# A hybrid decoder layer on one core: moving work from VectorE and GpSimd to ScalarE and to accumulating DMAs, and turning the attention-value product round

## The chip, the cores and the metric

The kernel runs on one core of a Trainium2 chip. The metric is device time in microseconds, the median of repeated runs. One further execution was taken by the hardware profiler; all rows below come from it.

## The reference

One layer works on a residual stream x of 1024 positions by 1024 channels. A conditioning vector c gives six vectors (shift, scale and gate for two sub-layers). The first sub-layer normalises x and makes one projection into state-space channels, eight query heads, two key heads and two value heads:

```python
h = _rms(x, norm1_w) * (1 + sc1) + sh1
u, q, k, v = split(h @ w_in)
y_ssm = _s5(u, ...)          # 32 groups, complex state of 64, scan over positions, GELU, GLU
y_attn = _swa_sink(rms(q), rms(k), v, rel_bias, sinks)   # 8 heads, window of 128, blocks of 128
mixed = concat([_rms(y_ssm, out_norm_ssm), _rms(y_attn, out_norm_attn)])
x = x + g1 * (mixed @ w_out)
h2 = _rms(x, norm2_w) * (1 + sc2) + sh2
x = x + g2 * _conv_ffn(h2, w_up, conv_w, conv_b, w_down)   # width 3 convolution, SiLU gate
```

The attention's softmax divides each row of exponentials by its sum plus the exponential of a learned sink:

```python
probs = p / (sum(p) + exp(sink - m));  out = probs @ v_band
```

## The kernel before

The residual stream is kept transposed: channels on partitions, positions on columns, in eight tiles x[0] to x[7] of 128 by 1024. A half h is 512 positions. All large matmuls run as `mm3` (line 143): each operand is split into a rounded part and a remainder (`split`, line 137), and three products are summed in one PSUM bank. In a split, one engine writes the rounded part (ScalarE unless named otherwise) and another the remainder (VectorE unless named otherwise). Helpers such as `tt`, `stt`, `cpy` issue most instructions, so a line of the profile (L118, L127, L133, L135, L97, L99) is often that of a helper, and the tiles tell the groups apart.

The stages in order of time are these. The adaLN vectors are made by VectorE (`emit_mod`, line 178), which reduces a loaded tile of w_mod against c (L180). The state-space input U is projected, and `emit_ut` (line 539) transposes it in eight groups of four 128-column blocks into one PSUM bank each, from where VectorE moves it to SBUF and adds a bias Bu (L118, tA<-bk,Bu). The heads' projections and the scan follow, the scan on VectorE. The scan's outputs go through a GELU on ScalarE, are transposed by TensorE into eight banks and moved to the tile zT (line 735, tS<-bk, four by ScalarE and four by VectorE). They are split (line 746, the rounded part by VectorE, tA<-tS) and pass the GLU (L770, L775).

Attention (lines 810 to 856) runs over eight blocks n of 128 queries and two key heads kv, in 16 units u. A unit makes the logits of four heads (tXQ,tH), adds the bias and takes the row maximum on VectorE (L828), takes exponentials on ScalarE with the row sum (L837), and takes the reciprocal of the sum plus sink (L840). Then P is multiplied by that reciprocal, on GpSimd in 14 units and on VectorE in two (the list `PM`; tH<-tH,att). P is transposed (cn,tH or cn,tA), the transposes are moved to PT by ScalarE or VectorE in turn (the list `EP`; tH<-bk, 15 of 30 by each), and the product with V follows:

```python
pe.matmul(av[kv * 64:kv * 64 + 64, :], vtok[...64 columns...], PT[:, kb * 512:kb * 512 + 512], ...)
```

V is stationary (64 columns) and the transposed probabilities of four heads move (512 columns), so channels come out on partitions. Each block's result is moved by two ScalarE copies of 128x256 (tU<-bk). P has three buffers, H4, H5 and A12.

After four blocks `branch_norm(h)` (line 788) normalises the attention branch: four squares on ScalarE, three sums on VectorE, a matmul with ones, a reciprocal square root over 128x512, four products on VectorE, four splits.

`proj` (line 882) makes one 128x512 piece of the output projection and adds it, times the gate g1, to x by one VectorE instruction (L127, tX<-bk,mod,tX or tXQ<-bk,mod,tXQ). Line 863 has loaded x before, in eight transfers of 512 KB issued by SyncE. The state-space share (br_i = 0) comes first, in the order d = 4 to 7 with both halves and then d = 0 to 3 with the first half; the second halves of d = 0 to 3 follow later. Its pieces use bank 5 for the first half and bank 6 for the second. The weights come through one staging buffer, W0. The attention share is added by `attn_out` (line 986) with `proj(d, h, 1, ...)`, which also stores x to DRAM and takes squares; `rms` (line 1003) normalises for the second sub-layer.

The order on each engine is made by a scheduler that simulates the kernel; attention has raised priority (line 807), and `attn_out` for the first half is held behind the last unit's reciprocal (line 1017). From there TensorE's order is that of the program text (L99, against L97 before). Sixteen `emit_mod` of the second sub-layer are held behind units 10 to 15 (the list `MOD_AT`, line 906). Each queue is served in its order, DMA issues included. The second sub-layer then keeps TensorE busy to the end.

## Time and profile before

| what | value |
|---|---|
| median of 3 runs | 1140.12 us (1139.39 to 1141.47) |
| the profiled execution's own time | 1142.15 us |
| span of the profiled execution | 1140.3 us |
| mean granted TensorE clock | 0.958 of full speed |

In the rows, PE is TensorE, PEld its weight loads, DVE is VectorE, ACT is ScalarE, POOL is GpSimd, SP is SyncE. "bk" is a PSUM bank. A busy time is the time in which an instruction of the engine, or of the group, was running; successive instructions overlap a little, so a mean times a count exceeds it slightly. PEclk is the mean granted clock, 1.00 for 2.4 GHz and 0.50 for 1.2 GHz. One 32-bit matmul appears as two records. A GpSimd instruction's span includes time in which it could not get on.

### The profile page before, as it was taken

The page shows a single profiled execution, that of the slowest core. Times are in us where ns is not written, and L with a number is a line of the kernel's source. Part 1 is how long each engine was busy: PE and PEld are TensorE (multiplying, and loading weights), DVE is VectorE, ACT ScalarE, POOL GpSimd, SP SyncE. Part 2 cuts the span into 40 slices and gives each one's busy share as a digit, 9 for nine tenths or more (in the row PEclk, how much of TensorE's full clock was granted, in tenths as well). Part 3 has the DMA queues.
Part 4 walks back from the last instruction along what each step waited for, and adds up shares of the span by engine and source line. Part 5 has one row for each costly group of instructions (what it writes and reads, how often), then busy time and mean ns, then how long its engine had stood idle before and what let it go on. Part 6 is the DMA issues. An engine that isn't in the chain of part 4 may idle for free.

```text
span 1140.3 us, 13281 instructions
## 1 busy us (share of the span) xinstructions
PE 1053.4 (92%) x4692; PEld 828.2 (73%) x4692; DVE 957.5 (84%) x1541; ACT 550.2 (48%) x936; POOL 256.7 (23%) x137
## 2 busy tenths in 40 slices
PE   6979999688989899779999999999999989989998
PEld 4868777475646577657888888888888768768876
DVE  8996899969988988888777878797777787997985
ACT  5412443583874346745554545455444554434342
POOL 0000000002121001762122223212212142353541
PEclk9979999679989899989999999999999989999999
DMA  9501516025024743222223232423123359120002
GB/s 371 214 19 39 127 40 93 1 88 190 19 94 183 240 147 112 93 92 93 93 78 113 87 130 93 151 90 112 56 93 126 115 217 384 63 93 1 1 37 111
DMA packets 47333, 128.13 MB, mean 112 GB/s; under 512 B 6017, under 2 KB 13985, under 8 KB 47266
## 3 DMA queue, kind: packets, MB, share of 16 engines
q1 hardware_dynamic: 47266, 127.28, 32.8%
q8 instruction: 37, 0.61, 0.2%
q14 instruction: 30, 0.25, 0.1%
HBM read 105.28 MB, written 21.99 MB: 112 GB/s over the span
## 4 chain that ended last, share of the span: by engine, by line
PE 60%; DVE 29%; ACT 4%; DMA 3%; issue 3%; POOL 1%; SPq 0%; ACTq 0%; DVEq 0%; POOLq 0%
PE bk L97 54%; PE bk L99 6%; DVE tA L118 5%; DVE tU L118 3%; DVE tH L118 3%; DVE tS L118 2%; DVE tX L127 2%; DMA tW<-in_dram 2%; DVE bk L118 2%; DVE tS L180 1%; DVE tXQ L118 1%; DVE tXQ L127 1%; DVE tX L118 1%; DVE tX L180 1%; ACT tU L133 1%
## 5 line engine op out<-in xcount | busy, mean ns | idle before, releaser
L97 PE MATMUL bk<-tU,tU 128*128 128x512 f32 x516 | 124.9, 395 | 4.8 <-DVE tXQ L127 2.4
L97 PE MATMUL bk<-tA,tU 128*128 128x512 f32 x516 | 128.1, 395 | 0.8 <-DVE tA L118 0.8
L97 PEld LDWEIGHTS bk<-tU,tU 128*128 128x128 f32 x516 | 97.6, 190 | 27.8 <-issue 2.8
L97 PE MATMUL bk<-tH,tU 128*128 128x512 f32 x477 | 116.0, 392 | 0.0
L97 PEld LDWEIGHTS bk<-tA,tU 128*128 128x128 f32 x516 | 96.7, 188 | 24.2 <-DVE tA L118 1.4
L127 DVE SCALAR_TENSOR_TENSOR tX<-tH,sm,tX 128x1023 f32<-128x1023 f32 x66 | 100.5, 1523 | 8.0 <-ACT tX L1097 7.9
L97 PEld LDWEIGHTS bk<-tH,tU 128*128 128x128 f32 x477 | 89.1, 188 | 19.3
L97 PE MATMUL bk<-tA,tXQ 128*128 128x512 f32 x300 | 76.0, 401 | 2.1 <-ACT tH L1050 2.1
L118 POOL TENSOR_TENSOR tU<-tW,tU 128x512 fp32r<-128x512 f32 x25 | 36.3, 1462 | 174.1 <-ACT tU L133 152.4
L97 PE MATMUL bk<-tH,tA 128*128 128x512 f32 (+1 forms) x168 | 63.9, 509 | 11.4 <-ACT tH L133 7.6
L133 ACT CAST tU<-tW 128x512 fp32r<-128x512 f32 (+1 forms) x67 | 47.1, 710 | 48.9 <-PE bk L97 18.2
L97 PEld LDWEIGHTS bk<-tA,tXQ 128*128 128x128 f32 x300 | 57.4, 191 | 16.0 <-ACT tH L1050 2.5
L99 PE MATMUL bk<-tH,tU 128*128 128x512 f32 x267 | 64.0, 395 | 1.8 <-DVE tU L118 1.7
L118 POOL TENSOR_TENSOR tH<-tH,att 128x1024 f32<-128x1024 f32 (+1 forms) x9 | 19.1, 2124 | 195.8 <-DVE att L840 161.7
L118 DVE TENSOR_TENSOR tX<-tX,tX 128x512 f32<-128x512 f32 (+1 forms) x63 | 61.6, 981 | 0.8
L118 POOL TENSOR_TENSOR tXQ<-tW,tXQ 128x512 fp32r<-128x512 f32 x12 | 49.1, 4102 | 53.1 <-ACT tXQ L133 37.8
L99 PEld LDWEIGHTS bk<-tH,tU 128*128 128x128 f32 x267 | 49.6, 189 | 15.6 <-DVE tU L118 2.7
L97 PE MATMUL bk<-tXQ,tH 128*128 128x256 f32 (+2 forms) x224 | 51.9, 374 | 4.3 <-DVE att L828 4.3
L118 DVE TENSOR_TENSOR tU<-tW,tU 128x512 fp32r<-128x512 f32 (+2 forms) x43 | 37.8, 881 | 20.4 <-ACT tU L133 20.4
L97 PEld LDWEIGHTS bk<-tXQ,tH 128*128 128x128 f32 x224 | 45.1, 268 | 13.3 <-DVE att L828 9.0
L118 POOL TENSOR_TENSOR tU<-tX,tU 128x512 fp32r<-128x512 f32 x19 | 33.2, 1747 | 84.9 <-ACT tU L133 70.8
L118 DVE TENSOR_TENSOR tU<-tX,tU 128x512 fp32r<-128x512 f32 x39 | 31.3, 808 | 23.6 <-ACT tU L133 23.6
(349 smaller groups left out, 2398.9 us busy)
## 6 DMA issues: line engine op xcount, KB each, us to landing
tX<-in_dram SPq DMA_DIRECT2D x51, 512.0 KB, 3.3
tW<-in_dram SPq DMA_DIRECT2D x49, 512.0 KB, 3.3
tS<-in_dram SPq DMA_DIRECT2D x30, 512.0 KB, 6.0
gd<-tX SPq DMA_DIRECT2D x22, 512.0 KB, 2.9
tA<-in_dram SPq DMA_DIRECT2D x12, 512.0 KB, 9.7
tH<-in_dram SPq DMA_DIRECT2D x12, 512.0 KB, 4.2
tH<-gd SPq DMA_DIRECT2D x8, 512.0 KB, 4.7
tA<-gd SPq DMA_DIRECT2D x8, 512.0 KB, 8.9
```

What stands on the lines that cost most here:

```text
L97: return f(*a, **k)
L99: i = f(*a, **k)
L118: return eng.tensor_tensor(out=o, in0=a, in1=b, op=op)
L127: return vec.scalar_tensor_tensor(out=o, in0=a, scalar=s, in1=b, op0=op0, op1=op1)
L133: act.copy(o, i)
L180: vec.tensor_tensor_reduce(out=st, in0=st, in1=ca, scale=1.0, scalar=S("b_mod", j, 1), op0=MUL, op1=ADD, accum_out=mod[:, j:j + 1],)
```

## The change

The change does six things. First, the eight bias moves of `emit_ut` go from one VectorE instruction each to four ScalarE instructions of 128x128. Second, in the list `PICK` all eight moves to zT go to ScalarE, the eight rounded parts of zT's split too, and of the 30 moves to PT VectorE keeps three. Third, P is no longer multiplied by the reciprocal; the product with V has PT as the stationary operand (128 columns) and V moving (64 columns), in eight matmuls a unit (four in the first two), so queries come out on partitions, and one VectorE instruction of 128x512 a block multiplies by the reciprocals. ScalarE then takes the row sum of squares into a junk output in the second unit's P buffer. Fourth, `branch_norm` works from these sums: a reciprocal square root over 128x4, four ScalarE scalings, 16 transposes into bank 7 (first half) or banks 0 to 3, and from the bank four ScalarE moves and four VectorE remainders. Fifth, `proj` for the state-space share writes g1 times the product to x by ScalarE, and a DMA issued by GpSimd adds the 256 KB of x from DRAM to it, in 16 transfers. Sixth, the eight loads of x by SyncE are gone.

```diff
-    "EI": "a", "EK": "a", "EP": "avavavavavavavavavavavavvaav", "ET": "a", "EU": "avaaavaa", "EV": "a", "EW": "a",
-    "EZ": "av", "NS0": "a", "NS1": "aav", "PM": "pppvppppp", "QH": "a", "ZH": "v", "YB": "67566556",
+    "EI": "a", "EK": "a", "EP": "aaaaaaaav", "EU": "avaaavaa", "EV": "a", "EW": "a",
+    "EZ": "a", "NS0": "a", "NS1": "aav", "QH": "a", "ZH": "a", "YB": "67566556",
...
-        tt(vec, v4[0], v4[1], Bu[:, 4 * i:4 * i + 4].rearrange("p (g o) -> p g o", o=1).to_broadcast([128, 4, 128]), ADD)
+        for q in range(4):
+            g = 4 * i + q
+            act.activation(out=UTt[i // 2][:, (g % 8) * 128:(g % 8 + 1) * 128], in_=b[:, q * 128:(q + 1) * 128], func=AF.Identity, bias=Bu[:, g:g + 1])
...
     def branch_norm(h):
...
+        ssq, rs, tm = [att[:, 128 * h + 4 * z:128 * h + 4 * z + 4] for z in range(3)]
+        rsqrt_mean(rs, tm, ssq, 512)
+        for j in range(4):
+            act.activation(out=Y[h][j], in_=Y[h][j], func=AF.Identity, scale=rs[:, j:j + 1])
         for m in range(4):
+            b = bank[m if h else 7]
+            for j in range(4):
+                pe.transpose(b[:, j * 128:(j + 1) * 128], Y[h][j][:, m * 128:(m + 1) * 128], ident)
+            hi, lo = mx[4 + m, h] = half(newr(f"H{8 + 4 * h + m}"))
+            act.activation(out=hi.r, in_=b, func=AF.Identity, scale=bw[:, 4 + m:5 + m])
+            stt(lo.r, b, bw[:, 4 + m:5 + m], hi.f, MUL, SUB)
...
-            tt(ENG[pick("PM", u)], P, P, rd.rearrange("p (i o) -> p i o", o=1).to_broadcast([128, 4, w_]), MUL)
...
-            for kb in range(nb):
-                blk = (n - 1 + kb) if n else 0
-                pe.matmul(av[kv * 64:kv * 64 + 64, :], vtok[:, blk * 128 + kv * 64:blk * 128 + kv * 64 + 64],
-                          PT[:, kb * 512:kb * 512 + 512], start=(kb == 0), stop=(kb == nb - 1))
+            for i in range(4):
+                for kb in range(nb):
+                    blk = (n - 1 + kb) if n else 0
+                    pe.matmul(av[:, (2 * i + kv) * 64:(2 * i + kv) * 64 + 64], PT[:, kb * 512 + i * 128:kb * 512 + i * 128 + 128],
+                              vtok[:, blk * 128 + kv * 64:blk * 128 + kv * 64 + 64], start=(kb == 0), stop=(kb == nb - 1))
...
+        tt(vec, g8[0], g8[1], att[:, 256 + 8 * n:264 + 8 * n].rearrange("p (g o) -> p g o", o=1).to_broadcast([128, 8, 64]), MUL)
+        act.activation(out=Pt[:, 0:512], in_=y, func=AF.Square, accum_out=att[:, 128 * (n // 4) + n % 4:128 * (n // 4) + n % 4 + 1])
...
-    for k in range(8):
-        sync.dma_start(out=x[k], in_=xT[k])
...
+        if br_i == 0:
+            i = act.activation(out=x[d][:, hs], in_=b, func=AF.Identity, scale=g1)
+            pol.dma_start(out=x[d][:, hs], in_=xT[d][:, hs], accum_op=ADD)
+            return i
         return stt(x[d][:, hs], b, g1, x[d][:, hs], MUL, ADD)
```

## Rows read from the trace of the kernel before

**Rows 1.** The page: busy time of each engine, and the ending chain by engine.
```profile
PE 1053.4 (92%) x4692; PEld 828.2 (73%) x4692; DVE 957.5 (84%) x1541; ACT 550.2 (48%) x936; POOL 256.7 (23%) x137
...
PE 60%; DVE 29%; ACT 4%; DMA 3%; issue 3%; POOL 1%; SPq 0%; ACTq 0%; DVEq 0%; POOLq 0%
```

**Rows 2.** Windows: stretch, its length, busy PE, PEld, DVE, ACT, POOL, PEclk, DMA.
```profile
94.00:111.00 17.00, 16.24 (x133) 13.97 (x133) 12.09 (x36) 5.35 (x9) 0.00 (x0) 1.00 0.12 39
...
235.00:257.00 22.00, 16.66 (x103) 13.71 (x102) 13.18 (x37) 18.98 (x51) 2.17 (x3) 0.77 0.35 120
257.00:273.00 16.00, 11.90 (x55) 7.24 (x52) 16.00 (x43) 3.48 (x13) 1.80 (x1) 1.00 0.53 178
273.00:330.00 57.00, 50.56 (x213) 33.14 (x214) 51.54 (x127) 44.37 (x113) 15.44 (x7) 0.88 0.19 62
330.00:382.00 52.00, 51.57 (x217) 31.92 (x215) 44.43 (x100) 23.82 (x61) 10.57 (x4) 1.00 0.54 191
382.00:402.00 20.00, 14.68 (x52) 10.76 (x52) 17.75 (x33) 7.66 (x12) 0.00 (x0) 0.83 0.73 239
402.00:457.00 55.00, 53.43 (x231) 42.96 (x231) 45.78 (x64) 30.92 (x47) 5.70 (x4) 1.00 0.36 126
```

**Rows 3.** Groups of VectorE, 235 to 400 us: busy, mean ns, idle before.
```profile
L135 DVE COPY tH<-bk 128x512 f32<-128x512 f32 x15 | 10.2, 679 | 0.2 <-PE bk L97 0.2
L127 DVE SCALAR_TENSOR_TENSOR tS<-tU,tS 128x512 f32<-128x512 f32 x8 | 8.7, 1104 | 0.0
...
L127 DVE SCALAR_TENSOR_TENSOR tX<-bk,mod,tX 128x512 f32<-128x512 f32 x8 | 5.8, 742 | 4.1 <-PE bk L97 4.1
...
L135 DVE COPY tS<-bk 128x512 f32<-128x512 f32 x4 | 4.4, 1104 | 2.7 <-PE bk L97 2.7
...
L135 DVE CAST tA<-tS 128x512 fp32r<-128x512 f32 x8 | 3.0, 417 | 1.6 <-ACT tS L133 1.6
```

**Rows 4.** The timeline of GpSimd and VectorE: start, length, instruction, idle before.
```profile
289.51 2.16 POOL L118 TENSOR_TENSOR tH<-tH,att 128x1024 f32<-128x1024 f32 x1 [7.75 <-DVE att L840]
...
289.84 2.38 DVE L127 SCALAR_TENSOR_TENSOR tS<-tU,tS 128x512 f32<-128x512 f32 x1
...
469.29 31.15 POOL L118 TENSOR_TENSOR tXQ<-tW,tXQ 128x512 fp32r<-128x512 f32 x1 [5.30 <-ACT tXQ L133]
```

**Rows 5.** The timeline of TensorE and VectorE near 390 us.
```profile
387.79 2.95 PE L97 MATMUL bk<-tA,tHA 128*128 128x512 f32 x12
395.98 4.85 PE L97 MATMUL bk<-tA,tHA 128*128 128x512 f32 x12 [5.24 <-DVE tXQ L127]
...
395.18 0.74 DVE L127 SCALAR_TENSOR_TENSOR tXQ<-bk,mod,tXQ 128x512 f32<-128x512 f32 x1
```

**Rows 6.** Groups of ScalarE, 235 to 400 us: busy, mean ns, idle before.
```profile
L133 ACT COPY tH<-bk 128x512 f32<-128x512 f32 x15 | 8.7, 580 | 6.5 <-PE bk L97 6.0 <-ACT tU L133 0.5
...
L770 ACT ACTIVATE tU<-bk,bg 128x512 f32<-128x512 f32 x8 | 5.3, 675 | 0.5 <-PE bk L97 0.5
...
L133 ACT COPY tU<-bk 128x256 f32<-128x256 f32 x16 | 5.1, 372 | 9.1 <-PE bk L97 9.1
...
L133 ACT COPY tS<-bk 128x512 f32<-128x512 f32 x4 | 4.4, 1095 | 0.0
L133 ACT CAST tU<-tW 128x1024 fp32r<-128x1024 f32 x3 | 3.1, 1048 | 10.0 <-DMA tW<-in_dram 10.0
```

**Rows 7.** The timeline of TensorE's 32-bit matmuls (stationary 128*64 or 128*128, then moving).
```profile
284.93 1.93 PE L97 MATMUL bk<-tH,tA 128*64 128x512 f32 x4
...
240.10 0.39 PE L97 MATMUL bk<-tA,tS 128*128 128x128 f32 x2
240.32 0.39 PE L97 MATMUL bk<-tHB,tA 128*128 128x128 f32 x2
```

**Rows 8.** DMA issues, 230 to 470 us: count, KB each, median us to landing.
```profile
tXQ<-in_dram SPq DMA_DIRECT2D x4, 512.0 KB, 5.2
...
xd<-tX SPq DMA_DIRECT2D x8, 256.0 KB, 2.1
```

More of the change, by code (lines that the diff above doesn't have):

```diff
@@ L38 @@
 PICK = {
-    "EI": "a", "EK": "a", "EP": "avavavavavavavavavavavavavvaav", "ET": "a", "EU": "avaaavaa", "EV": "a", "EW": "a",
-    "EZ": "av", "NS0": "a", "NS1": "aav", "PM": "pppvppppp", "QH": "a", "ZH": "v", "YB": "67566556",
+    "EI": "a", "EK": "a", "EP": "aaaaaaaav", "EU": "avaaavaa", "EV": "a", "EW": "a",
+    "EZ": "a", "NS0": "a", "NS1": "aav", "QH": "a", "ZH": "a", "YB": "67566556",
 }
@@ L545, in emit_ut @@
             pe.transpose(b[:, q * 128:(q + 1) * 128], U[:, g * 128:(g + 1) * 128], ident)
-        v4 = [a_.rearrange("p (g c) -> p g c", g=4) for a_ in (UTt[i // 2][:, (i % 2) * 512:(i % 2 + 1) * 512], b)]
-        tt(vec, v4[0], v4[1], Bu[:, 4 * i:4 * i + 4].rearrange("p (g o) -> p g o", o=1).to_broadcast([128, 4, 128]), ADD)
+        for q in range(4):
+            g = 4 * i + q
+            act.activation(out=UTt[i // 2][:, (g % 8) * 128:(g % 8 + 1) * 128], in_=b[:, q * 128:(q + 1) * 128], func=AF.Identity, bias=Bu[:, g:g + 1])
     for i0, n_ in ((0, 4), (4, 2), (6, 2)):
@@ L788, in branch_norm @@
     def branch_norm(h):
-        src = [yT[h][i // 2][:, i % 2, :] for i in range(4)]
-        tg_ = (("U4", "U5"), ("H4", "H5"))[h]
-        (acc, sq), (rs, yt) = half(new(tg_[0])), half(new(tg_[1]))
-        act.activation(out=acc, in_=src[0], func=AF.Square)
-        for m in range(1, 4):
-            act.activation(out=sq, in_=src[m], func=AF.Square)
-            tt(vec, acc, acc, sq, ADD)
-        b = bank[(7, 0)[h]]
-        pe.matmul(b, ones, acc, start=True, stop=True)
-        rsqrt_mean(rs, yt, b, 512)
-        for m in range(4):
-            yo = (yt, sq)[m % 2]
-            stt(yo, src[m], bw[:, 4 + m:5 + m], rs, MUL, MUL)
-            mx[4 + m, h] = half(newr(f"H{8 + 4 * h + m}"))
-            split(mx[4 + m, h], yo)
+        ssq, rs, tm = [att[:, 128 * h + 4 * z:128 * h + 4 * z + 4] for z in range(3)]
+        rsqrt_mean(rs, tm, ssq, 512)
+        for j in range(4):
+            act.activation(out=Y[h][j], in_=Y[h][j], func=AF.Identity, scale=rs[:, j:j + 1])
+        for m in range(4):
+            b = bank[m if h else 7]
[4 more added lines that the diff above has]
+            stt(lo.r, b, bw[:, 4 + m:5 + m], hi.f, MUL, SUB)
     hp = ctx.enter_context(ExitStack())
     hp.enter_context(tc.high_priority(0))
-    yT = [[new(f"U{2 * h + j}").rearrange("p (i t) -> p i t", i=2) for j in range(2)] for h in range(2)]
+    Y = [[y for j in range(2) for y in half(new(f"U{2 * h + j}"))] for h in range(2)]
     att = pool.tile([128, 16 * 20], F32, name="att")
@@ L815, in hymba_kernel @@
             k0 = (n - 1) * 128 if n else 0
-            P = new(("H4", "H5", "A12")[u % 3])[:, 0:4 * w_].rearrange("p (i j) -> p i j", i=4)
+            Pt = new(("H4", "H5", "A12")[u % 3])
+            P = Pt[:, 0:4 * w_].rearrange("p (i j) -> p i j", i=4)
             PT = new(("H6", "H7")[u % 2])
-            m_, ng, su, es, rd = [att[:, 20 * u + 4 * z:20 * u + 4 * z + 4] for z in range(5)]
+            m_, ng, su, es = [att[:, 16 * u + 4 * z:16 * u + 4 * z + 4] for z in range(4)]
+            rd = att[:, 256 + 8 * n + kv:264 + 8 * n:2]
             for i2 in range(2):
@@ L847, in hymba_kernel @@
                 evac(PT[:, kb * 512:kb * 512 + 512], b, "P")
-            for kb in range(nb):
-                blk = (n - 1 + kb) if n else 0
-                pe.matmul(av[kv * 64:kv * 64 + 64, :], vtok[:, blk * 128 + kv * 64:blk * 128 + kv * 64 + 64],
-                          PT[:, kb * 512:kb * 512 + 512], start=(kb == 0), stop=(kb == nb - 1))
-        for j in range(2):
-            evac(yT[n // 4][j][:, :, (n % 4) * 128:(n % 4) * 128 + 128],
-                 av[:, 256 * j:256 * j + 256].rearrange("p (i q) -> p i q", i=2), "T")
+            for i in range(4):
[3 more added lines that the diff above has]
+                              vtok[:, blk * 128 + kv * 64:blk * 128 + kv * 64 + 64], start=(kb == 0), stop=(kb == nb - 1))
+        y = Y[n // 4][n % 4]
+        g8 = [a_.rearrange("p (g d) -> p g d", g=8) for a_ in (y, av)]
+        tt(vec, g8[0], g8[1], att[:, 256 + 8 * n:264 + 8 * n].rearrange("p (g o) -> p g o", o=1).to_broadcast([128, 8, 64]), MUL)
+        act.activation(out=Pt[:, 0:512], in_=y, func=AF.Square, accum_out=att[:, 128 * (n // 4) + n % 4:128 * (n // 4) + n % 4 + 1])
         if n % 4 == 3:
```

## The prediction

> **What bounds the kernel now.** I read the page's engine line first, then the windows, then the groups and the timeline of the stretch that the change touches. The page says that TensorE is busy 92% and VectorE 84% of the span, and that the ending chain is 60% TensorE and 29% VectorE [rows 1]. These are averages over stages, so the windows decide. From 402 us on TensorE is busy 53.4 of 55 us and later as densely: nothing taken from another engine can be won there. From 235 to 402 us, where the scan's output, GLU, attention and first projections lie, the five windows add up to 167 us with VectorE busy 142.9, TensorE 145.4 and ScalarE 98.3 [rows 2]. In 257 to 273 us VectorE has no pause at all. TensorE's 145.4 holds time at a lower clock: the granted clock is 0.77, 0.88 and 0.83 in three of the windows, so part of them ran at 1.2 GHz instead of 2.4. So VectorE leads this stretch, TensorE is close behind, and ScalarE has room.
>
> Two details say why. While a GpSimd multiplication of P runs (2.16 us from 289.51), a VectorE instruction that starts beside it takes 2.38 us [rows 4]; a move of the same size takes 0.679 [rows 3]. And near 391 us TensorE stands 5.24 us until a projection's VectorE instruction of 0.74 us, begun at 395.18, has freed the bank [rows 5].
>
> **The change, part by part, from 235 to 402 us. VectorE.** Durations are group means [rows 3]. It loses twelve of the sixteen projection pieces (8.9 us at 0.742), twelve moves to PT (8.1 at 0.679), four moves to zT (4.4 at 1.104) and eight rounded parts (3.3 at 0.417). The two P multiplications of 1024 columns are no row of mine; at two moves of 512 each they are 2.7. The first branch_norm loses 13 instructions of 128x512 and gains four from a bank: 13 x 0.679 - 4 x 0.742 = 5.8. Eight multiplications by the reciprocals come in: 8 x 0.679 = 5.4. With GpSimd's 14 multiplications goes what they cost VectorE: at least 3.4 (eight instructions with a mean of 1.104 against 0.679), at most 14 times the 1.70 of the one instruction in [rows 4], 23.8; I take 10, since only some of the 14 meet such an instruction. Together VectorE loses 37.8 and is left with 105.1.
>
> **ScalarE.** It gains four moves to zT (4.4 at 1.095), eight rounded parts and twelve moves to PT at 0.58 (11.6), twelve projection pieces at the 0.675 of an activation from a bank (8.1) and eight squares at the same price (5.4). It loses sixteen half moves (6.0 at 0.372) and about two instructions of the branch norm (1.2) [rows 6]. That is 22.3 more, 120.6 in all.
>
> **TensorE.** The product with V was 30 matmuls, 60 records, at 1.93/4 = 0.48 us: 29.0. Now it is 120 matmuls, 240 records, with 128 stationary and 64 moving columns. The nearest rows have 128 of each and start 0.22 us apart for two [rows 7], so 0.11 a record; if moving columns set that, 64 take 0.055 and the sum is 13.2, if stationary columns do, it is 26.4. I take 26.4, because the stationary operand is as in the row. The Trainium skill, TensorE: Matmul & The Clock Gate, section LDWEIGHTS, says that loading goes by the number of stationary columns at 1.2 per ns; by that, an estimate of 25.6, and by moving columns the end would come up to 13 us earlier, which no run here shows yet. Sixteen transposes come in (1.8 at 0.11) and one sum with ones goes (two records, 1.0). Net: 1.8 less. The time at the low level is at most 2 x (1 - clock) x window = 30.6 us, of which at most the 21.6 idle us were not work; so 9.0 to 30.6 us of work ran at 1.2 GHz, and feeding TensorE steadily gives back half, 4.5 to 15.3. I take 8, near the lower end, since the pauses lie in the same windows. That leaves 135.6, bounds 128 and 141.
>
> **The stretch.** TensorE is then the longest, ScalarE second, VectorE third. Fed well, TensorE is 0.97 to 0.99 busy, in 273 to 330 us 0.89 [rows 2]. I take 0.90, because P, its transposes and PT still go round three engines: 135.6/0.90 = 150.7, 16.3 us less than 167. The ends are 132 (128 at 0.97) and 158 (141 at 0.89), gains of 35 and 9. The pause of 5.24 us is part of this: the move that ends it is now ScalarE's, which is 38% busy in that window.
>
> **The edits outside.** In emit_ut eight groups of four ScalarE instructions come into 94 to 111 us. A group costs at least 0.58 and at most 4 x 0.372 = 1.49; I take 1.2, as small instructions are nearer the second. ScalarE's 5.35 us become 15 of 17 [rows 2, 6], but TensorE's transposes wait for these banks and it has 0.8 us to spare, and the scan starts behind: a loss of 1 us, bounds 0 and 3. VectorE's own 5 us there buy nothing, as it pauses already. The four later projection pieces and the second branch_norm lie beside a TensorE that is 97% busy, so I cost them at nothing; without that cover they would give back up to 9 us.
>
> **The transfers.** Eight loads leave SyncE's queue, 16 come into GpSimd's, in front of which only its idle time stands; the remainders that it makes for the second sub-layer come later. Bytes from DRAM are the same. Issue to landing lies between 2.1 us (a store of 256 KB) and twice the 5.2 of a 512 KB load, as each adds a read of its target [rows 8]; I take 4, near the row of equal size. The page DMA: Bandwidth & Descriptors of the Trainium skill, section Anatomy of one DMA, gives a fixed 2.0 us plus bytes, an estimate of 2.6. The third first-half piece ends its matmuls at 390.7; its reader needs two more groups of twelve, 5.9 us [rows 5]. Move (0.7), issue (1) and landing (4) are 5.7, so it is just hidden. At 10.4 and a GpSimd issue of 2.2 the reader would be 7.4 late, everything on VectorE behind it as well, but TensorE has two more banks, 5.9 us, before it stands: at most 1.5 us. SyncE's gain I take as none, as the loads were issued early.
>
> **Sum.** 16.3 - 1 = 15.3 off 1142.15, the profiled execution's own time: 1126.9. The median is 2.0 below that execution, so I predict **1125 us**.
>
> **The rivals.** *TensorE fed better, or the product by moving columns.* About 131 us of work at 0.94 is 139, 28 off, less 1: 1113. For it: VectorE's 105 leaves slack everywhere. Against it: the dependencies within a unit.
>
> *ScalarE becomes the bound.* It already works 44.4 of 57 us in 273 to 330 us, a share of 0.78, where exponentials wait on VectorE, and it stood 10.0 us waiting for weights in front of three casts [rows 2, 6]; a projection's move queued behind such a cast holds a bank. 120.6/0.78 = 155, with half of those 10 us, 160: 7 off, less 1, 1134. If its share falls to 0.73 or less, nothing is won.
>
> *Slower: the accumulating transfers land late.* One mechanism: GpSimd must make the transfers, and it can be kept from working by VectorE. Its one instruction at 469.29 took 31.15 us beside a VectorE that ran without a pause [rows 4]. If the first transfers are held so, the reader in VectorE's queue waits 31.2 instead of 5.7 us, with 5.9 covered by banks: some 20 us, and 1142.15 - 15.3 + 20 - 2.0 = 1145. It decides from about 27 us from move to landing. Against it: VectorE is 89% busy where these transfers start, and less after the change. The Trainium skill, SBUF — State Buffer, section SBUF: two separate sides, warns of just this: a DMA issued by GpSimd waits while VectorE's two-port instructions keep it from writing descriptors; the trace's 31 us agrees that GpSimd can be locked out, but no row shows it for a transfer.
>
> *The change moves the bank pauses elsewhere* is no case of its own: it is the far end of ScalarE's.
>
> **How the numbers follow.** About 0.2% (2.3 us) can be told from no change. The forecast gets 0.48, the better case 0.17, ScalarE 0.22 (0.14 faster, 0.08 within the 0.2%), late transfers 0.13. So faster 0.79, same 0.08, slower 0.13. The forecast's own range is 1117 to 1132. The range 1108 to 1142 takes in most of the better case and all of ScalarE's, and leaves out the late transfers and the best end.
>
> **What would show it.** Right: no GpSimd multiplication; VectorE near 105 us and ScalarE near 121 between the last GELU and the first half's attention projections; the 5.24 us pause gone; TensorE at 0.90 or more in this stretch; the second sub-layer as long as before. Wrong: VectorE's adds of the attention share waiting for DMAs; TensorE waiting for ScalarE's moves with ScalarE idle before weight casts; records of the product with V clearly under 0.11 us or above; the scan starting more than 3 us later.

## The result and the profile after

The changed kernel takes **1146.96 us** (median of 4 runs, 1146.28 to 1148.07) against 1139.76 before: ratio **1.0063, interval 1.0049 to 1.0076**, so it is slower by 0.6%. The prediction was 1125, range 1108 to 1142. The profiled execution took 1146.35 us, with a span of 1144.1.

The page of the changed kernel, its engines' line, its transfer queues and its ending chain:

```profile
PE 1055.2 (92%) x4900; PEld 853.3 (75%) x4900; DVE 912.6 (80%) x1485; ACT 581.2 (51%) x1008; POOL 240.8 (21%) x139
...
q1 hardware_dynamic: 46114, 123.09, 31.7%
q0 software_dynamic: 2304, 4.20, 2.3%
...
PE 58%; DVE 26%; ACT 7%; DMA 4%; issue 3%; POOL 0%; SPq 0%; ACTq 0%; DVEq 0%
```

Against [rows 1] VectorE lost 45 us of work, ScalarE gained 31, and TensorE, which was to do less, does 1.8 us more. The stretch from 235 to 402 us as one window, and the two windows behind it:

```profile
235.00:402.00 167.00, 149.29 (x868) 125.79 (x867) 104.33 (x291) 116.29 (x278) 10.54 (x12) 0.95 0.43 126
...
402.00:457.00 55.00, 49.46 (x205) 38.77 (x203) 41.67 (x65) 34.19 (x53) 6.45 (x6) 0.94 0.55 164
457.00:512.00 55.00, 40.11 (x141) 30.18 (x142) 45.83 (x69) 30.01 (x52) 40.73 (x8) 0.81 0.30 100
```

The columns are start and end, length, then busy time and instructions of PE, weight load, DVE, ACT and POOL, the granted clock, the transfers' share and GB/s. VectorE fell from 142.9 to 104.3 and ScalarE rose from 98.3 to 116.3 [rows 2], as forecast, in a stretch in which nothing was to get longer. From 402 to 457 TensorE now has 5.5 idle us instead of 1.6 [rows 2].

Windows with fixed ends cannot say what became shorter. These begin and end at the same pieces of work, the first start to within 0.2 us: the last y matmul of the scan, the start of the state-space share of the second half (bk<-tA,tHB on L99), the first product of the second sub-layer with an A5 operand, the end. First the kernel before, then the changed one:

```profile
240.70:418.18 177.48, 155.86 (x656) 104.44 (x654) 156.13 (x350) 104.48 (x256) 29.98 (x14) 0.91 0.42 141
418.18:502.06 83.88, 69.51 (x282) 53.91 (x280) 72.28 (x108) 49.23 (x81) 44.03 (x10) 0.92 0.32 109
502.06:1140.30 638.24, 618.09 (x2641) 499.08 (x2639) 517.57 (x618) 298.53 (x458) 182.12 (x108) 0.99 0.29 106
```

```profile
242.60:416.18 173.58, 153.34 (x843) 127.12 (x842) 114.45 (x302) 121.98 (x288) 10.54 (x12) 0.94 0.47 140
416.18:510.44 94.26, 76.35 (x297) 58.79 (x296) 74.71 (x107) 54.24 (x89) 47.18 (x14) 0.87 0.37 109
510.44:1144.10 633.66, 614.41 (x2641) 496.69 (x2639) 516.99 (x617) 299.00 (x458) 182.57 (x107) 0.99 0.29 106
```

This is the whole balance. The start is 1.9 us later, the stage of GLU, attention and first projections is 3.9 shorter, the next is **10.4 longer**, and the second sub-layer gives 4.6 of that back: 1.9 - 3.9 + 10.4 - 4.6 = 3.8, the difference of the spans. In the first stage TensorE's idle time fell only from 21.6 to 20.2 us. The stage that grew is one that the prediction costed at nothing. TensorE's timeline in it:

```profile
416.18 2.97 PE L99 MATMUL bk<-tA,tHB 128*128 128x512 f32 x12
418.99 0.93 PE L97 MATMUL bk<-cn,tU 128*128 128x128 f32 x7
419.67 3.04 PE L99 MATMUL bk<-tA,tHB 128*128 128x512 f32 x12
422.55 0.38 PE L97 MATMUL bk<-cn,tU 128*128 128x128 f32 x2
422.76 1.02 PE L99 MATMUL bk<-tH,cn 128*128 128x512 f32 x2
423.22 6.17 PE L99 MATMUL bk<-tA,tHA 128*128 128x512 f32 x24
429.23 0.93 PE L97 MATMUL bk<-cn,tU 128*128 128x128 f32 x7
...
432.29 0.73 PE L99 MATMUL bk<-tH,tU 128*128 128x512 f32 x2 [2.13 <-ACT tU L133]
433.55 23.09 PE L99 MATMUL bk<-tH,tU 128*128 128x512 f32 x94 [0.53 <-DVE tU L118]
```

The transposes of Y for the second branch norm (bk<-cn,tU) are strewn between the projections, and seven stand behind the 24 matmuls of tHA. Y lies in U2 and U3, the slot into which the first weights of the second half go, so these are split late and TensorE waits 2.13 and 0.53 us. That attention share began at 430.28 before and ran without a pause; now it begins at 432.29 and has no further pause from 433.55.

The waits are not the whole 10.4 us. The same later pieces, first before, then in the change:

```profile
430.28 21.92 PE L99 MATMUL bk<-tH,tU 128*128 128x512 f32 x96
453.15 0.73 PE L99 MATMUL bk<-tS,tU 128*128 128x512 f32 x2 [0.95 <-ACT tU L133]
454.51 2.60 PE L99 MATMUL bk<-tS,tU 128*128 128x512 f32 x10 [0.63 <-POOL tU L118]
```

```profile
458.65 0.73 PE L99 MATMUL bk<-tS,tU 128*128 128x512 f32 x2 [2.00 <-ACT tU L133]
460.01 4.12 PE L99 MATMUL bk<-tS,tU 128*128 128x512 f32 x10 [0.63 <-POOL tU L118]
```

The same ten matmuls take 4.12 us instead of 2.60 behind the pauses, and the 94 above take 23.09 where 96 took 21.92; the stage's mean granted clock is 0.87 instead of 0.92, so more of it ran at 1.2 GHz instead of 2.4. Added up along the stage, about 1.9 us are the transposes themselves, 3.5 are longer waits and 5.0 are the same matmuls running longer at the lower clock.

The other steps: the transfers that add landed near the time that was taken, and no VectorE instruction waited for one. Issues by tile, median us to landing:

```profile
tX<-in_dram POOLq DMA_DIRECT2D x8, 256.0 KB, 4.7
tXQ<-in_dram POOLq DMA_DIRECT2D x8, 256.0 KB, 4.6
```

### The profile page after: what moved, and what is told of

Same layout as the page of the kernel before. It is cut to its first block, busy times and chain, and to the rows that moved or that the text cites. A ratio compares the mean times of both kernels' runs of the same rounds, so it can differ in the third digit from the quotient of the medians.

```text
span 1144.1 us, 13672 instructions
## 1 busy us (share of the span) xinstructions
PE 1055.2 (92%) x4900; PEld 853.3 (75%) x4900; DVE 912.6 (80%) x1485; ACT 581.2 (51%) x1008; POOL 240.8 (21%) x139
## 3 DMA queue, kind: packets, MB, share of 16 engines
q1 hardware_dynamic: 46114, 123.09, 31.7%
q0 software_dynamic: 2304, 4.20, 2.3%
## 4 chain that ended last, share of the span: by engine, by line
PE 58%; DVE 26%; ACT 7%; DMA 4%; issue 3%; POOL 0%; SPq 0%; ACTq 0%; DVEq 0%
PE bk L97 53%; DVE tA L118 5%; PE bk L99 5%; DVE tU L118 3%; DVE tH L118 3%; DVE tS L118 2%; DVE tX L127 2%; DMA tW<-in_dram 2%; DVE bk L118 2%; DVE tXQ L127 1%; DMA tS<-in_dram 1%; DVE tXQ L118 1%; ACT tU L133 1%; DVE tX L180 1%; ACT tH L836 1%
## 5 line engine op out<-in xcount | busy, mean ns | idle before, releaser
L97 PE MATMUL bk<-tH,tU 128*128 128x512 f32 x477 | 115.9, 392 | 0.0
L127 DVE SCALAR_TENSOR_TENSOR tX<-tH,sm,tX 128x1023 f32<-128x1023 f32 x66 | 100.3, 1519 | 8.2 <-ACT tX L1099 8.0
L97 PEld LDWEIGHTS bk<-tH,tU 128*128 128x128 f32 x477 | 89.1, 188 | 19.2
L99 PE MATMUL bk<-tH,tU 128*128 128x512 f32 x267 | 69.7, 415 | 9.6 <-ACT tU L133 6.1
L99 PEld LDWEIGHTS bk<-tH,tU 128*128 128x128 f32 x267 | 51.9, 199 | 24.2 <-ACT tU L133 7.5
L118 DVE TENSOR_TENSOR tX<-tX,tX 128x512 f32<-128x512 f32 (+1 forms) x63 | 61.6, 982 | 1.2 <-DMA tX<-in_dram 0.3
L118 POOL TENSOR_TENSOR tU<-tW,tU 128x512 fp32r<-128x512 f32 x25 | 36.6, 1475 | 122.7 <-ACT tU L133 101.0
L118 POOL TENSOR_TENSOR tXQ<-tW,tXQ 128x512 fp32r<-128x512 f32 x12 | 48.9, 4084 | 53.1 <-ACT tXQ L133 37.9
L887 POOL DMA_DIRECT2D tX<-in_dram x8 | 7.1, 885 | 244.2 <-DVE tA L118 221.6
L118 DVE TENSOR_TENSOR tU<-tW,tU 128x512 fp32r<-128x512 f32 (+2 forms) x43 | 37.9, 883 | 24.5 <-ACT tU L133 24.5
L97 PE MATMUL bk<-tXQ,tH 128*128 128x256 f32 (+2 forms) x224 | 49.6, 365 | 3.6 <-DVE att L827 3.5
L118 POOL TENSOR_TENSOR tU<-tX,tU 128x512 fp32r<-128x512 f32 x19 | 32.9, 1734 | 85.5 <-ACT tU L133 71.3
L118 DVE TENSOR_TENSOR tU<-tX,tU 128x512 fp32r<-128x512 f32 x39 | 31.3, 808 | 23.6 <-ACT tU L133 23.6
L97 PE MATMUL bk<-tH,tXQ 128*128 128x512 f32 x192 | 47.2, 395 | 0.0
```

The costliest lines, as they stand in the source:

```text
L97: return f(*a, **k)
L99: i = f(*a, **k)
L118: return eng.tensor_tensor(out=o, in0=a, in1=b, op=op)
L127: return vec.scalar_tensor_tensor(out=o, in0=a, scalar=s, in1=b, op0=op0, op1=op1)
L887: pol.dma_start(out=x[d][:, hs], in_=xT[d][:, hs], accum_op=ADD)
```

## The experiments

Each ratio is against the kernel before, run on the same chip. The runs were made on five chips, on which the kernel before had medians from 1138.7 to 1140.4 us. A difference between two changed kernels is given in medians; where the ratios tell it otherwise or their intervals overlap, the text says so. An edit that moves one step makes the scheduler lay the order of every later instruction down anew, so a reversal tests its own cost and a new order at once. The runs that set an order alone (in the second and third group) do the same work in another order.

### One part undone

*emit_ut back on VectorE.*

```diff
-        for q in range(4):
-            g = 4 * i + q
-            act.activation(out=UTt[i // 2]..., in_=b[:, q * 128:(q + 1) * 128], func=AF.Identity, bias=Bu[:, g:g + 1])
+        tt(vec, v4[0], v4[1], Bu[:, 4 * i:4 * i + 4]...to_broadcast([128, 4, 128]), ADD)
```

> The changed kernel with emit_ut alone put back on VectorE. The changed kernel measured 1147.0 us (1.0063 of the kernel before). In its trace the scan ends 2.0 us later (205.2 against 203.2 us) and TensorE waits several times for a tA written by ScalarE. Theory 1 (this delay is passed on to the end): 2 us less, about 1145.0, ratio 1.0045, and the scan ends near 203.2. Theory 2 (the delay is swallowed, because attention's last units and the weights for its projection come from other chains between 260 and 430 us): the scan ends 2 us earlier but the time stays within 0.7 us of 1147.0.

Measured 1134.21 us, ratio 0.9956 (0.9938 to 0.9974): 12.8 less than the change, where 2 was the most expected. Neither theory.

*zT and zs back.*

```diff
-    "EZ": "a", ... "ZH": "a",
+    "EZ": "av", ... "ZH": "v",
```

> The changed kernel with the moves to zT alternating between ScalarE and VectorE again and the rounded parts of zs back on VectorE (12 instructions, 7.7 us by the rows of before). In the changed kernel the first GLU product starts at 263.0 us against 257.1. Theory 1 (ScalarE bounds this stretch and its delay reaches the end): the first GLU product near 259, 4 us less, about 1143, ratio 1.0028. Theory 2 (the delay is regained before 330 us anyway; what sets the end is the reloading of one staging buffer for the output weights from 367 to 412 us and the second branch norm): GLU starts earlier, but the time stays within 1.5 us of 1147.0.

Measured 1135.58, ratio 0.9965 (0.9951 to 0.9978). That is more than the ScalarE theory asked for, and the time did not stay as the other theory had it. But the squaring is as late as in the change (325.2 us), while the norm's transposes end ahead of the sum with ones, so the gain may come at that later place: what the work before 330 us costs by itself is not shown here.

*The state-space share back on VectorE, x loaded by SyncE.*

```diff
-        if br_i == 0:
-            i = act.activation(out=x[d][:, hs], in_=b, ...)
-            pol.dma_start(out=x[d][:, hs], in_=xT[d][:, hs], accum_op=ADD)
-            return i
+    for k in range(8):
+        sync.dma_start(out=x[k], in_=xT[k])
```

> The changed kernel with the state-space share of the projection as before: x loaded by SyncE, a VectorE instruction that adds into it, no accumulating transfer. Late-transfer rival: the transfers cost what the change lost, so 6 us or more come back: 1141 or less, ratio 1.001 or less. Theory 2 (the transfers are hidden, and VectorE's four to nine us here are hidden too): within 2 us of 1147.0, ratio 1.0045 to 1.008. If VectorE's relief was worth something: 1150 to 1156.

Measured 1141.76, ratio 1.0016 (1.0004 to 1.0029): 5.2 less. That lies between the theories, but the traces of after show no wait for a landing, and here the norm's transposes end at 415 us, ahead of the sum with ones.

*The moves to PT alternating as before.*

```diff
-    "EP": "aaaaaaaav",
+    "EP": "avavavavavavavavavavavavavvaav",
```

> The changed kernel with the moves to PT alternating between ScalarE and VectorE as before (twelve moves, 7 us, back to VectorE). Theory 1 (ScalarE is the bound where TensorE waits for its move to PT, 321 us): 3 us less, about 1144, ratio 1.0037. Theory 2 (the end is set later, by the staging buffer and the second branch norm): within 1.5 us of 1147.0.

Measured **1130.40, ratio 0.9918** (0.9900 to 0.9936): 16.6 less. This kernel is the whole change but for twelve moves, and it comes near the forecast. All four reversals gain, by 5 to 17 us. This suggests that something in the changed kernel's order was bad and that each of them happened to mend it. In ScalarE's timeline the changed kernel has this place:

```profile
316.65 1.28 ACT L189 ACT_TABLE_LOAD   x1
317.95 0.69 ACT L189 ACTIVATE tW<-bk,sm 128x512 f32<-128x512 f32 x1
318.66 1.28 ACT L836 ACT_TABLE_LOAD   x1
319.95 0.51 ACT L836 ACTIVATE tH<-tH,att 128x256 f32<-128x256 f32 x1
...
321.63 1.28 ACT L189 ACT_TABLE_LOAD   x1
322.93 0.30 ACT L189 ACTIVATE att<-att,sm 128x4 f32<-128x4 f32 x1
323.24 1.28 ACT L836 ACT_TABLE_LOAD   x1
...
326.03 0.61 ACT L190 ACTIVATE tA<-tW 128x512 f32<-128x512 f32 x1
```

and with PT back the same place reads:

```profile
315.21 1.28 ACT L189 ACT_TABLE_LOAD   x1
316.51 0.30 ACT L189 ACTIVATE att<-att,sm 128x4 f32<-128x4 f32 x1
316.71 0.67 ACT L189 ACTIVATE tW<-bk,sm 128x512 f32<-128x512 f32 x1
317.28 0.19 ACT L190 ACTIVATE att<-att 128x4 f32<-128x4 f32 x1
317.41 0.63 ACT L190 ACTIVATE tA<-tW 128x512 f32<-128x512 f32 x1
```

The reciprocal root of GLU's second norm (tW<-bk) and that of the new branch norm (att<-att) each bring a table load, and another to return to exponentials. With PT back they share one pair. In the changed kernel they have two pairs, and GLU's squaring (L190) stands behind four exponentials of P, two moves to PT and the second pair of loads, 8 us late. The first state-space piece comes at 328.1 instead of 320.6, but it does not hang on this squaring: it is a piece of the first half, whose last remainders were made at 309.6. What hangs on it is the second half, whose splits begin at 333.7 instead of 324.4 and for which TensorE then waits:

```profile
307.09 2.49 DVE L118 TENSOR_TENSOR tA<-tS,tA 128x512 fp32r<-128x512 f32 x4
...
335.09 4.45 PE L97 MATMUL bk<-tA,tHB 128*128 128x512 f32 x18 [0.23 <-DVE tA L118]
```

The second place is the transposes at 419 to 430.

### One order set, and the weights' buffers

*The slots of the weights turned,* so that the second half's first pair does not need U2 and U3:

```diff
-    slots += [(("U4", "U5"), ("U2", "U3"), ("U0", "U1"))[i % 3] for i in range(5)]
+    slots += [(("U4", "U5"), ("U0", "U1"), ("U2", "U3"))[i % 3] for i in range(5)]
```

> The changed kernel with the weights' slots of attention's projection turned: the first pair of the second half goes into U0, U1 and the second into U2, U3, where it was the other way round. TensorE's order is nearly the same as in the changed kernel up to 430 us. Theory A (the second branch norm came late, keeps Y in U2, U3 until its last transposes at 429.2 us, and so holds the weights that TensorE then waits for, 2.13 and 0.53 us at 432): both waits go, and with U2, U3 free earlier also the 2.00 us at 458: 3 to 6 us less, 1141 to 1144, ratio 1.001 to 1.0035. Theory B (the loss was made before 330 us by ScalarE and only shows here): within 1 us of 1147.

Measured 1145.11, ratio 1.0040 (1.0026 to 1.0055): 1.9 less, between the two, and the intervals of this kernel and of the change overlap. In its trace the wait for weights at 432 is gone, but TensorE then waits 2.21 us for the norm's low part (tH L127). So the slot was at most the last link.

*The last product with V ahead of the projection,* an order on TensorE alone:

```diff
-                    pe.matmul(av[:, (2 * i + kv) * 64: ...
+                    lastav = pe.matmul(av[:, (2 * i + kv) * 64: ...
     pst.enter_context(pe.pin(True))
+    pe.last = lastav.ins
```

> The changed kernel with one order set: TensorE's first product of attention's projection comes after the last product with V (in the changed kernel the records of the last unit's product are strewn among the projection's from 372 to 398 us, and the chain of the second branch norm, y, squares, rsqrt, scaling, transposes, ends only at 430). Nothing else of the work changes. Theory A (that chain being late is what costs): the last y multiplication at about 386 instead of 404, the transposes before 415, no wait at 432: 5 us less, about 1142, ratio 1.002. Rival (the chain is late because VectorE and ScalarE are late, the order on TensorE is harmless): within 1 us of 1147, or slower, as the projection now starts later.

Measured 1141.87, ratio 1.0019 (1.0004 to 1.0033): **5.1 less, as expected.** The last y multiplication came at 391.78 instead of 404.00. TensorE's timeline there:

```profile
407.03 0.38 PE L97 MATMUL bk<-cn,tU 128*128 128x128 f32 x2
408.55 5.29 PE L99 MATMUL bk<-tH,tU 128*128 128x512 f32 x22 [1.14 <-DVE tU L118]
413.68 5.78 PE L99 MATMUL bk<-tA,tHB 128*128 128x512 f32 x24
419.98 1.13 PE L99 MATMUL bk<-tH,cn 128*128 128x512 f32 x2 [0.52 <-DVE tH L118]
420.54 6.18 PE L99 MATMUL bk<-tA,tHA 128*128 128x512 f32 x24
426.56 21.93 PE L99 MATMUL bk<-tH,tU 128*128 128x512 f32 x96
```

The norm's last transposes are over at 407, and the attention share follows the 24 matmuls of tHA without a pause, 5.7 us sooner. So the order that made the second norm late is shown to cost some 5 us. The trace holds only part of that gain: the profiled execution took 1144.71 us, 2.8 above the median, and TensorE waits 4.54 us for weights at 453.

*Two staging buffers* for the first four pairs of weights:

```diff
-        st = new("W0" if i < 4 else f"W{i % 2}")
+        st = new(f"W{(i + 1) % 2}" if i < 4 else f"W{i % 2}")
```

> The changed kernel with two staging buffers instead of one (W1 and W0 in turn) for attention's first four pairs of weights, so that a load need not wait for the split of the one before. Theory S (this staging sets the pace of the projection from 387 to 416 us, where TensorE waits 0.53, 0.53, 2.00 and 0.53 us for weights): these waits go, 3 us less, about 1144. Rival (the 16 DMA engines are 98% busy from 382 to 402 us, so that a second buffer only makes loads overlap and each slower): within 1 us of 1147.

Measured 1149.00, ratio 1.0079 (1.0067 to 1.0092), 2.0 more, with overlapping intervals: no gain, and a loss is not shown. The waits for weights did go (tHB began at 412.3 instead of 416.2), but TensorE then waited 4.4 us for the scaled Y (tU L793) and 3.3 for its low part. While the norm is late, faster staging only moves the wait to it.

*PT alternating with the last product first and the turned slots.*

> The changed kernel with the moves to PT alternating as before (alone 1130.4 us, 0.9918) and with both the order of the last product with V and the turned slots. If these two are worth what theory A says only where the second branch norm is late, and it is not late there (its transposes end at 413.3 before the sum with ones): 1 to 2 us less from the slots alone (the 1.19 us wait at 442.7), 1128 to 1130. If they add up in full: 1122 to 1125.

Measured 1140.00, ratio 1.0000 (0.9990 to 1.0010), 9.6 *more* than PT back alone. The norm's transposes were over at 394.6, but the low parts of the weights, also VectorE's, had come behind its steps: TensorE waits 5.5 us in all for tU L118 and 2.75 for the squares' sum. Here two edits were made at once, and which of them harms is not separated.

### The squaring ahead of the exponentials

*One order on ScalarE:* from unit 9 on, exponentials come behind the squaring of GLU's second norm, which `rsqrt_mean` now returns.

```diff
-        rsqrt_mean(rss, sq, b, 2048)
+        glu = rsqrt_mean(rss, sq, b, 2048)
-            with tc.issue_after(gelus[7]):
+            with tc.issue_after(glu if u >= 9 else gelus[7]):
```

> The changed kernel with one order set on ScalarE: the exponentials of attention's units 9 to 15 come after the squaring (L190) in GLU's second norm. In the changed kernel that squaring stands at 326.0 us, 8 us after the reciprocal root it belongs to (317.95), behind exponentials and a second pair of table loads that the new branch norm's own reciprocal root brings; in the two variants that gained most (emit_ut back, PT back) it comes at 317.4. Up to that place nothing in the order changes. Theory T (this place costs the 8 us by which the first state-space piece of the projection is late, 328.1 against 318.8 and 320.6): the piece starts near 320, two table loads less, and 5 to 8 us off, 1139 to 1142. Rival (the piece is early but the weights through the one staging buffer set the pace after 387 us): the piece starts near 320, the time within 1.5 us of 1147.

Measured 1143.76, ratio 1.0030 (1.0019 to 1.0040): 3.2 less. The squaring came at 320.26, 5.8 us sooner, the second half's splits at 326.4 instead of 333.7 and the first piece at 325.1, 3 us sooner: between the theories. Theory T took the first piece to wait for the squaring, which it does not. The norm's transposes were as late as in the change.

*Both orders.*

> The changed kernel with both orders set: the exponentials of units 9 to 15 after GLU's second squaring, and the projection's first attention product after the last product with V. The second alone gave 1141.9 us, 5.1 less than the change. If the two delays are separate and follow one another, they add up: 1134 to 1137. If both are the same 5 us seen twice: 1140 to 1142.

Measured 1139.81, ratio 0.9990 (0.9978 to 1.0003): 7.1 less (8.3 by the ratios), against 3.2 + 5.1 = 8.3. The delays are separate, and together they bring the change level with the kernel before. (Its profiled execution, 1134.3 us, is the shortest of its 12 runs.)

*The squaring's order with emit_ut back.*

> The changed kernel with the exponentials of units 9 to 15 after GLU's second squaring and emit_ut back on VectorE. With emit_ut back alone the time was 1134.2 us, and there the squaring came early by itself. Theory T: the 12.8 us that emit_ut gave are 2 us of its own (the scan's start) and the rest this order; so here 1133 to 1136, no better than emit_ut alone. If emit_ut itself was worth the 12.8 us and the order some 6 more: 1127 to 1129.

Measured 1136.45, ratio 0.9963 (0.9950 to 0.9976): no better than emit_ut back alone. With the scan only 1.9 us later in the change, this fits that most of the 12.8 us of that reversal was order.

*All three.*

> The changed kernel with emit_ut back on VectorE and both orders set (squaring before the exponentials of units 9 to 15, last product with V before the projection's first attention product). If the three delays add up: 1147 less 2, 7 and 5, so 1131 to 1134, below the kernel before (1140). If the second order costs as much as it gives where the norm is early already, as with PT back (1140.0 against 1130.4): 1138 to 1143.

Measured 1139.77, ratio 0.9997 (0.9988 to 1.0007): the second expectation. It is 3.3 us more than without the order on TensorE, clear of noise, so an order that mends one kernel harms another. The weights' low parts, VectorE's work, are late; TensorE waits 5.53 us for tU L118.

### What is left: buffers, PT, attention alone

*Both orders and two staging buffers.*

> The changed kernel with both orders set (1139.8 us) and two staging buffers. Alone the two buffers took the waits for weights out of the projection (the share with tHB began at 412.3 instead of 416.2), but TensorE then stood 4.4 us for the scaled Y of the second branch norm and 3.3 us for its low part, and the time was 1149.0. If the staging comes next once the norm is early: 3 to 5 us less, 1135 to 1137. Rival (the transfers share 16 engines that are nearly full, a second buffer gives nothing in any order): within 1.5 us of 1139.8.

Measured 1136.80, ratio 0.9981 (0.9970 to 0.9991). The median is 3.0 less, but on this chip the kernel before was 1.6 us faster too (1138.74 against 1140.37): by the ratios the gain is 1.0 us, and the intervals overlap. So a gain from the buffers is not shown, although the median fell where it was expected.

*PT alternating and two staging buffers.*

> The changed kernel with the moves to PT alternating (1130.4 us) and two staging buffers. There TensorE waits 3.07 us for weights at 391.8 and nothing else over 1.2 us up to 470. If that wait goes: 1127 to 1128. Rival (no gain, the load is slower or something else is late): 1129 to 1132.

Measured **1128.33, ratio 0.9910** (0.9895 to 0.9926), 2.1 less than PT back alone by the medians and 0.9 by the ratios, not clear of noise. In the trace the wait of 3.07 us is gone. The median is the lowest of all, level with the next.

*PT alternating and emit_ut back.*

> The changed kernel with the moves to PT alternating and emit_ut on VectorE, the two single reversals that gained most (1130.4 and 1134.2 us). If each has a cost of its own (the scan 2 us later with emit_ut on ScalarE): 1128 to 1129. If both gained mostly because the order was laid down anew, nothing adds up: 1129 to 1138.

Measured 1128.75, ratio 0.9908 (0.9892 to 0.9924): 1.7 less by the medians and 1.1 by the ratios. That fits a cost of emit_ut's own on ScalarE, but is not clear of noise either.

*Attention alone:* all of the change's other parts undone.

> Of the change only attention itself: the product with V turned round, the reciprocals multiplied into y, no multiplication on GpSimd, the new branch norm; emit_ut, zT, the projection's state-space share and the moves to PT as before. If this part carries the gain that the best reversal shows: 1130 to 1134. If the gain needs the moves, roundings and accumulating transfers too: 1137 or more.

Measured 1145.59, ratio 1.0052 (1.0033 to 1.0071). The turned product and the new branch norm by themselves lose about as much as the whole change, with the same late transposes (until 427.3, then a wait of 2.31 for the low part). They carry no gain in this order; whether they would with an early norm was not run.

*PT alternating, emit_ut back, two buffers.*

> The changed kernel with the moves to PT alternating, emit_ut on VectorE and two staging buffers. Against PT back alone (1130.4) the buffers gave 2.1 and emit_ut 1.7 us. If these are two separate costs: 1126 to 1127, the best of all. If the new order undoes one: 1128 to 1131.

Measured 1138.40, ratio 0.9985 (0.9976 to 0.9993): the sum did not come, and the time is above even the second range, 8 us or more above PT back with either part alone. In its trace the norm is late once more: eight transposes wait 6.31 us for the scaled Y at 413.77, eight stand at 422.71 behind the matmuls of tHA, and the attention share waits 3.30 us, at the place that the order on TensorE had shown.

*PT alternating, no accumulating transfers.*

> The changed kernel with the moves to PT alternating (1130.4 us) and the state-space share of the projection as before: no accumulating transfers, twelve more pieces on VectorE (8.9 us). In the changed kernel this reversal gave 5.2 us, but the second branch norm came early there by itself. If the transfers harm (late landing, or twice the transfer time per byte): 1127 or less. If they are hidden and VectorE's relief in this stretch is worth what the prediction said of the longest engine (VectorE is not the longest): within 2 us of 1130.4. If VectorE's relief is what lets the weights' low parts and the norm come early: 1134 or more.

Measured 1132.08, ratio 0.9935 (0.9921 to 0.9949): within 2 us of 1130.4, and not told from it. So the transfers do no harm that can be told here, and relieving VectorE of these pieces is worth little by itself.

### All runs side by side

Starts in us from the start of the profiled execution; the time is the median on the run's own chip, so differences of 2 us between rows say little. Some profiled executions lie off their median: slots turned 4.6 us above, last product first 2.8 above, both orders 5.5 below.

| kernel | squaring | last transposes of 2nd norm | sum with ones | attention share, 2nd half | time |
|---|---|---|---|---|---|
| before | 323.5 | none | 423.8 | 430.3 | 1139.8 |
| the change | 326.0 | 429.2 | 422.8 | 432.3 | 1147.0 |
| two buffers | 325.8 | 431.4 | 424.4 | 435.7 | 1149.0 |
| attention alone | 322.4 | 427.3 | 420.8 | 430.3 | 1145.6 |
| slots turned | 327.0 | 432.8 | 426.3 | 435.7 | 1145.1 |
| squaring first | 320.3 | 428.2 | 421.8 | 431.8 | 1143.8 |
| PT and emit_ut back, buffers | 314.7 | 422.7 | 415.5 | 427.0 | 1138.4 |
| last product first | 326.0 | 407.0 | 420.0 | 426.6 | 1141.9 |
| projection back | 325.2 | 414.2 | 423.5 | 430.1 | 1141.8 |
| PT back, last product, slots | 318.0 | 394.1 | 421.9 | 428.4 | 1140.0 |
| both orders | 320.2 | 401.6 | 415.3 | 421.9 | 1139.8 |
| both orders, emit_ut back | 319.8 | 399.2 | 424.9 | 431.3 | 1139.8 |
| both orders, buffers | 318.1 | 397.8 | 417.7 | 424.3 | 1136.8 |
| squaring first, emit_ut back | 317.9 | 417.6 | 418.0 | 424.5 | 1136.5 |
| zT back | 325.2 | 415.8 | 417.5 | 424.0 | 1135.6 |
| emit_ut back | 317.4 | 414.2 | 414.6 | 421.1 | 1134.2 |
| PT and projection back | 317.0 | 401.2 | 412.6 | 419.1 | 1132.1 |
| PT back | 317.4 | 411.4 | 413.1 | 419.6 | 1130.4 |
| PT and emit_ut back | 314.4 | 407.8 | 409.5 | 416.0 | 1128.8 |
| PT back, buffers | 317.2 | 406.9 | 410.1 | 416.7 | 1128.3 |

In these profiles, from the start of the attention share to the end takes 707 to 716 us in every kernel, 710 before and 712 in the change. That is 9 us of spread, against 20 in the start of that share: most is decided ahead of it. The first six below the kernel before have transposes behind the sum with ones; five of them are the five slowest of all, and the sixth is 8 us or more slower than its two relatives. Transposes ahead of it are not enough: with the projection back, or with the order on TensorE added to early norms, the share starts at 428 to 431 all the same.

## Why the prediction was wrong

**What held.** The load moved nearly as worked out: VectorE 104.3 in the stretch (105.1 predicted), ScalarE 116.3 (120.6). So close a hit is in part luck, as the fixed window holds other work after the change: between the same pieces of work VectorE lost 41.7 us (37.8 worked out) and ScalarE gained 17.5 (22.3). There was no GpSimd multiplication of P, and the pause of 5.24 us of [rows 5] was gone. GpSimd's issues took 0.87 us (1 taken) and the transfers landed after 4.6 to 4.7 us (4 taken): hidden, and never held by VectorE. So the slower rival as written is out, although the outcome is on its side and within 2 us of its 1145. The Trainium skill, SBUF — State Buffer, section SBUF: two separate sides, warns that VectorE can keep GpSimd from writing the descriptors of a transfer that it issues; no run here shows it. emit_ut was to cost 1 us (0 to 3): the stage behind it starts 1.9 us later.

**The product with V** came out by the price of the stationary operand, the reading that I took. Sixteen records of the changed kernel, that is one unit's product:

```profile
381.77 1.89 PE L97 MATMUL bk<-tA,tH 128*128 128x64 f32 x16
```

That is 0.118 us each, against 0.11 for the row with twice the moving columns [rows 7], so 240 make 28.4 us at that pace (26.4 taken). The Trainium skill, TensorE: Matmul & The Clock Gate, section LDWEIGHTS, counts the loading by stationary columns, and the 0.118 us agree with that. A fixed cost per record would look the same: no run changes the stationary columns beside 64 moving ones.

**The first step that failed: "the stretch", 16.3 us.** The stage gave 3.9, so 12.4 are missing. I took TensorE's work as 135.6 at a share of 0.90. The share was 0.89 in the fixed window, but because more time was busy, not because the stage was shorter: from last y matmul to the second half's state-space share the work fell by 2.5 us (9.8 taken, 8 of it from the clock) and the idle time by 1.4. What the idle time hangs on, in the product's group over that stage, first the kernel before, then the change:

```profile
L97 PE MATMUL bk<-tH,tA 128*64 128x512 f32 x60 | 33.5, 659 | 4.7 <-ACT tH L133 3.2 <-DVE tH L135 1.3 <-ACT tU L133 0.2
```

```profile
L97 PE MATMUL bk<-tA,tH 128*128 128x64 f32 x240 | 32.3, 281 | 8.0 <-ACT tH L133 6.5 <-DVE tU L118 1.3
```

With the moves to PT on ScalarE TensorE waits 6.5 us for them there; before, it waited 3.2 for those on ScalarE and 1.3 for those on VectorE. This is the rival "ScalarE becomes the bound", given 0.22, which named the mechanism (a move queued behind other work) but priced it by ScalarE's total, which was never the limit: 122 busy us of 173.6. What counted was its order. With PT back and two buffers the same stage and the same group are:

```profile
242.00:400.97 158.97, 149.53 (x846) 128.25 (x845) 114.72 (x303) 107.27 (x264) 10.51 (x12) 0.92 0.50 147
```

```profile
L97 PE MATMUL bk<-tA,tH 128*128 128x64 f32 x240 | 33.9, 288 | 4.0 <-DVE tH L135 3.0 <-ACT tH L133 0.9
```

159.0 us, 18.5 less than before, with 9.4 us idle instead of 21.6. So a gain of the size of the 16.3 was there for nearly this work in another order, and 12.2 of it are idle time and 6.3 busy time, where the prediction had put 9.8 on the work, 8 of them on the clock. (Its upper bound for the work, 141, does not follow from its terms: 143.6 less 4.5 is 139.1. The forecast does not hang on it.)

**The second: the second branch norm "at nothing", because TensorE is 97% busy there.** That was read from the window that ends at 457 us, and "later as densely" was misread: in the next one before, TensorE is busy 42.2 of 55 us.

```profile
457.00:512.00 55.00, 42.21 (x166) 32.34 (x165) 47.25 (x73) 30.37 (x53) 38.41 (x6) 0.88 0.29 95
```

Where it does run without pauses it has no gaps in which added matmuls could hide: 16 transposes went into an order that is fixed from there on, and with them a chain of y, squares, root, scaling, transposes and low parts through three engines, ahead of weights that need Y's tiles. The stage grew by 10.4 us: the transposes 1.9, waits 3.5, the lower clock behind them 5.0. The second sub-layer gave 4.6 back, 3.3 of them up to 545 us, where the kernel before had waited 2.11 us for an operand and the change waits 0.87. Setting one order gave 5.1, nearly the remaining 5.8.

The terms add up: 12.4 + 5.8 + 0.9 (emit_ut) = 19.1, the distance of the spans from the forecast -15.3 to the measured +3.8. The other 3 us to 22.0 are the median against the profiled execution (2.0 below it before, 0.6 above it after) and 0.4 outside the span.

**What stays open.** Two orders are shown, 7.1 us together (8.3 by the ratios), which is what the change lost against the kernel before; the gain that was forecast on top of that is not accounted for by them. A third cost, the moves to PT on ScalarE, is seen in the waits before the product: 8.0 us in the change and 4.7 with PT back, of them 6.5 and 1.5 for ScalarE. That the rest of the 16.6 us of PT back is this cost, and not one more accident of order, was not separated: no run holds the order and changes the engine of these moves alone.

## What to carry to other kernels

Where a scheduler lays out the order, the time of an edit is its own cost plus that of a new order: here kernels with the same work, but for a few moves, lay between 1128 and 1149 us. Judge such a change by undoing its parts one at a time, compare each version with the kernel before on the same chip, and compare traces between pieces of work, not between times. A step added beside an engine that is 97% busy is not hidden by it, above all if it holds a buffer that the next stage needs; follow its chain to the tile it frees.

## What was not expected of the hardware

An accumulating transfer took the transfer engines about twice as much per byte here. Queue q0 moved its 4.20 MB in 2.3% of 1144.1 us, 26.3 us of all 16 engines, or 6.3 us per MB; q1 moved 123.09 MB in 31.7%, 2.9 us per MB. The plain loads of the same bytes that the change took out had used about 11 us of q1 (32.8% of 1140.3 us before). The accumulating ones were cut into twice as many packets, 2304 against 1152; how much of the difference is that is not separated. The Trainium skill's page DMA: Bandwidth & Descriptors, section Anatomy of one DMA, had given an estimate of 2.6 us for its landing; measured are 4.6 to 4.7.

A matmul record of 64 moving columns took no less than one of 128 beside the same stationary size (0.118 and 0.11 us a record), so turning the product round saved only 1.2 us of TensorE's time (33.5 to 32.3 in the groups above), with four times as many records.
